# The first stage of a decoder step in another fixed order: loads issued by GpSimd, squares, responses and first GLU weights placed elsewhere

## The chip, the cores and the metric

The kernel runs on one core of one Trainium2 chip. The metric is the device time of one execution in microseconds (us), the median of the runs; lower is better. Engines are named as in the profile: PE is TensorE (PEld its weight loads), DVE is VectorE, ACT is ScalarE, POOL is GpSimd, SP is SyncE. SPq, ACTq and POOLq are the three sequencers as issuers of DMAs; each has a DMA queue of its own, and all queues share 16 DMA engines.

## The reference, cut to what matters

One inference step over 320 tokens (256 of a prompt, 8 sequences of 8 samples), model width 1024. Layer 0 mixes with a state space model (S5), layer 1 with latent attention; each then attends into 256 memory tokens and applies an MLP. The change lies in the S5 mixer and in the keys and values of layer 0's memory, which the kernel computes beside it.

```python
abar_re = mag * jnp.cos(ai * dt); abar_im = mag * jnp.sin(ai * dt)
bbar_re = coef_re[..., None] * br - coef_im[..., None] * bi     # and bbar_im
bu_re = jnp.einsum('gnk,btgk->btgn', bbar_re, ug)               # ug: rms_norm(x), 64 groups of 16
# h[t] = abar * h[t-1] + bu[t], for every group and state
y = jnp.einsum('gkn,btgn->btgk', cr, h_re) - jnp.einsum('gkn,btgn->btgk', ci, h_im)
y = y.reshape(bsz, t, dm) + d_skip * u
z = jax.nn.gelu(y, approximate=False) @ w_glu
out = z[..., :dm] * jax.nn.sigmoid(z[..., dm:])
k = (rms_norm(mem_prompt) @ w_mem_k); v = (rms_norm(mem_prompt) @ w_mem_v)
```

## The kernel before, in words

The tokens are cut into 40 chunks of 8 (`NCH`; 32 of the prompt, one for each sample). Inside a chunk the S5 layer is a short convolution (its *responses*, spread into the triangular tile `tt`); between chunks the state runs on in a scan. The 64 groups are treated in four quarters `hq` of 16. The pieces are small functions inside `s5_scan`, and the list of their calls is the order of the stage:

- `load_x` loads x (`xc`) and C (`natc`); C is cut into rows of 64 numbers. `mem_load` loads the memory tokens (`mt`), `mem_block(j)` turns one eighth of them into `mnp`.
- `products(i)`, i from 0 to 15: 16 matmuls of `mnp` with a 512 KB piece of the key or value weights; four pieces `i` are in flight, `products(i)` issues the load of piece i + 4 on SP. `keys(g)`, `keys_turned(g)`, `keys_out(g)` and `values_out(g)` copy the results out of PSUM, turn them and send them off through two halves of a buffer `kvo` (shown as `wlo`).
- The squares of x (`squares(i)`, 8 of them) give the norm of x; `x_scaled(i)` applies it, `x_turned(n)` turns x into `U`.
- `turned('b', q)`, `turned_out('b', q, p)` turn B, and the same with `'c'` turns C (PSUM tile `bcps`, results `m_b` and `m_c`).
- `state_weights(hq, hh)` on DVE and `state_turned(hq, hh)` on PE and ACT make the weights from chunk to state (`rt`), `states(hq)` applies them (`sps`). `out_weights(hq, hh)` on DVE makes the weights from state to output (`ca`, `ct`).
- `responses(hq)` fills a PSUM tile `kps`; `responses_out(hq)` copies it to the only buffer `kk` with four instructions of ACT, adds a diagonal on POOL, and spreads it to `tt` with 8 DMAs on SP. `kk` is free again when these have landed.
- `scan(f)` and `scanned(f)` run the scan of half the groups on DVE and copy it to `HS`. `outputs(hq, half)` multiplies `tt`, `ca`, `ct` by `U` and `HS` into a PSUM tile `yps`; ACT copies that to `yc` or `yg`; `outputs_turned`, `outputs_high` and `outputs_low` make the GLU's input. The dense GLU follows; its weights come in chunks through `load_chunk` (DMA, then `whi` on ACT and `wlo` on DVE).

PSUM has three rings: `mm` of 4 tiles (`products`, turned keys), `tp` of 2 (turns), and `at` of 2, which `rps`/`dps`, `ups`, `sps`, `kps` and `yps` take in turn. A tile of a ring is free when its reader has copied it out.

`in_order` ties every instruction of `s5_scan` to the one traced before it on the same engine, so that PE, DVE, ACT and SP run the list as written; what is traced later (the GLU's chunks) is put between by the scheduler. An engine whose next instruction waits holds back all behind it, and a DMA issue that cannot go on holds its sequencer.

Of the kernel before, what the change touches and what calls it, by code (L numbers as in the profile page):

```python
# [88 lines left out]
class Trunk:  # L89
# [88 lines left out]
    def load_chunk(self, srcs, cols):  # L178

        nc = self.nc  # L180
        if self.chunks_ahead:
            return self.chunks_ahead.pop(0)
# [12 lines left out]
        return hi, lo  # L195

# [412 lines left out]
    def s5(self, mkv):  # L609
        sp, close_sp = self.open("s5")  # L610
        mn, close_mn = self.open("memn0", side="right")
        with self.in_order((mybir.EngineType.PE, mybir.EngineType.DVE, mybir.EngineType.Activation, mybir.EngineType.SP)):
# [7 lines left out]
    def glu_chunk(self, k0):  # L620
        Wv = self.I['w_glu'][0].rearrange("(k p) c -> p k c", p=128)
        return self.load_chunk([(lambda t, o=o: t.rearrange("p (k c) -> p k c", c=512)[:, :, o * 256:(o + 1) * 256],
                                 Wv[:, k0:k0 + 2, o * D:o * D + 256]) for o in range(2)], 1024)

    def glu_loads(self, group):
        if group == 1:
            self.keys_scaled()
# [30 lines left out]
    def s5_scan(self, sp, mkv, mn):  # L658
# [39 lines left out]
        def load_x():  # L698
            for i in range(2):
                cols = slice(i * D // 2, (i + 1) * D // 2)  # L700
                A.dma_start(xc[i * NCH:i * NCH + NC_P], I['x_prompt'][0].rearrange("(c s) d -> c s d", s=L)[:, :, cols])
                A.dma_start(xc[i * NCH + NC_P:(i + 1) * NCH], I['x_sample'][:, :, cols])
            for i, part in enumerate(('re', 'im')):
                for o in range(2):
                    A.dma_start(nat['c'][i * G:(i + 1) * G, :, o], I[f'ssm_c_{part}'][0])

# [8 lines left out]
        PQ.dma_start(cm, I['c_chunk'])  # L715
        self.mem_load(0, mkv)
# [88 lines left out]
        T2 = pp.tile([128, 8, G], F32, name="T2")  # L805
        U = sp.tile([128, G * NCH + 24], F32, name="U")
# [4 lines left out]
        V.memset(tts[0], 0.0)  # L811
# [22 lines left out]
        load_x()  # L834
# [18 lines left out]
        A.activation(tts[1].rearrange("p s u k -> p (s u k)"), tts[0].rearrange("p s u k -> p (s u k)"), AF.Copy)  # L853
# [25 lines left out]
        A.activation(nat['b'][:, :, 1], nat['b'][:, :, 0], AF.Copy)  # L879
# [15 lines left out]
        def turned_out(c, q, p):  # L895
            A.activation(mat[c].rearrange("p r g k -> p k r g")[:, q * 4:q * 4 + 4],
                         p.rearrange("p (k r g) -> p k r g", k=4, r=2), AF.Copy)

        keys(0)
# [7 lines left out]
        for i in range(L):  # L907
            squares(i)
# [16 lines left out]
        V.tensor_add(rev(QX), T1, T2)  # L925
        V.tensor_mul(T1, Y1[:, :L], cb(cor))
# [32 lines left out]
        state_weights(0, 0)  # L959
        p = [turned('c', 0), turned('c', 1)]  # L960
        turned_out('c', 0, p[0])
        turned_out('c', 1, p[1])
        keys(1)
        ps = at("rps")
        products(4, lambda: nc.tensor.matmul(ps[:2 * NCH, :L], cm, rn[:, 0], start=True, stop=True))
        A.activation(rn[:, 1], ps[:2 * NCH, :L], AF.Sqrt, bias=self.eps[:2 * NCH, 0:1], scale=1.0 / D)
        A.activation(rm[:, 1], rm[:, 0], AF.Sqrt, bias=self.eps[:, 0:1], scale=1.0 / D)
        p = [turned('c', 2), turned('c', 3)]
        turned_out('c', 2, p[0])
        turned_out('c', 3, p[1])  # L970
        state_turned(0, 0)
        a8n = sp.tile([128, 2, G], F32, name="a8n", tag="a8n", bufs=1)
        A.activation(a8n[:, 0], PR[:, 8], AF.Copy)
        A.activation(a8n[:, 1], PI[:, 8], AF.Copy)
        for t, v in ((X1, PI), (Y1, PR)):
            A.activation(t[bot], v[bot], AF.Copy, scale=-1.0)
        state_weights(0, 1)
        V.reciprocal(rC, rn[:, 1])
        V.reciprocal(rm[:, 0], rm[:, 1])
# [13 lines left out]
        for i in range(4):  # L993
            x_scaled(i)
        products(5)
        state_turned(0, 1)
        for i in range(4, L):
            x_scaled(i)
        state_weights(1, 0)
        keys(2)  # L1000
        PQ.tensor_mul(dn, dn, gxn[:G])
# [5 lines left out]
        products(6)  # L1007
        V.tensor_copy(dT, ps[:K, :G])
        V.tensor_copy(rB, ps[:, 128:384])
        state_turned(1, 0)  # L1010
        state_weights(1, 1)
        keys_turned(0)
        for n in range(4):
            x_turned(n)
        state_turned(1, 1)
        for n in range(4, 8):
            x_turned(n)
        close_par()
# [1056 lines left out]
```

## Time and profile before

| | |
|---|---|
| time, median of 3 runs | 1228.91 us (1224.6 to 1232.43) |
| the profiled execution: time, span | 1227.92 us, 1226.3 us |
| PE busy over the span | 1131.8 us (92%) |
| DVE, ACT, POOL busy | 701.9, 555.9, 65.8 us |
| chain that ended last | PE 82%, ACT 6%, DVE 6%, DMA 3% |

The span is what the trace covers, and the time has 1.6 us more around it. The chain that ended last is read from the end back, each piece to what released it. "Idle before" names what an engine waited for.

### The profile page before, as it was taken

Reading aid. Unit: us, or ns where it says so; the run is one execution under the profiler, and the core shown is the slowest. Engines: PE = TensorE matmul, PEld = TensorE weight load, DVE = VectorE, ACT = ScalarE, POOL = GpSimd, SP = SyncE. Lnnn points to the kernel's source line nnn. Section 1 sums busy time; section 2 is a strip of 40 time slices with the busy share of each in tenths; the row PEclk is TensorE's granted clock in tenths of the full one; section 3 lists DMA queues with packets and bytes.
Section 4 is the critical chain, followed back from the end, with each engine's and each line's share of the span. In section 5 each row is a group of like instructions: output and inputs, shape, how many; then the busy total and the mean of one; then the engine's idle time right before and its main releaser. Section 6 shows DMA issues by size and latency. Waiting matters only on the chain.

```text
span 1226.3 us, 21300 instructions
## 1 busy us (share of the span) xinstructions
PE 1131.8 (92%) x8233; PEld 1025.4 (84%) x8233; DVE 701.9 (57%) x1327; ACT 555.9 (45%) x1012; POOL 65.8 (5%) x110
## 2 busy tenths in 40 slices
PE   2898869999899999999999999999998999999995
PEld 1787669986598999999988985569966899999995
DVE  2787944494358643564587584326852675335553
ACT  2764545444345543453375353324443465335531
POOL 0011100000000000000000054200000000000000
PEclk7998979999999999999999999989999999999998
DMA  8235259755434444554462654537561434444541
GB/s 203 87 83 138 36 130 292 272 189 189 174 118 130 152 155 143 150 154 148 147 186 74 171 179 139 168 137 248 182 232 61 137 109 149 146 148 139 168 141 43
DMA packets 152738, 185.38 MB, mean 151 GB/s; under 512 B 19824, under 2 KB 120445, under 8 KB 152573
## 3 DMA queue, kind: packets, MB, share of 16 engines
q1 hardware_dynamic: 140812, 173.00, 45.9%
q10 hardware_dynamic: 8592, 5.47, 1.9%
q0 software_dynamic: 3232, 5.55, 1.4%
q8 instruction: 65, 1.06, 0.4%
q14 instruction: 37, 0.30, 0.1%
HBM read 175.41 MB, written 6.21 MB: 148 GB/s over the span
## 4 chain that ended last, share of the span: by engine, by line
PE 82%; ACT 6%; DVE 6%; DMA 3%; issue 1%; SPq 1%; POOL 0%; POOLq 0%; ACTq 0%; DVEq 0%
PE mm L218 19%; PE mm L217 19%; PE mm L219 19%; PE mm L742 2%; PE kt L102 2%; PE sps L1451 2%; PE s L1934 2%; ACT whi L192 2%; PE ops L1466 1%; PE pov L1508 1%; PE s L1975 1%; DMA natc<-in_ssm_c_re 1%; DVE wlo L193 1%; PE ltp L102 1%; PE pps L1486 1%
## 5 line engine op out<-in xcount | busy, mean ns | idle before, releaser
L193 DVE TENSOR_TENSOR wlo<-wraw,whi 128x1024 fp32r<-128x1024 f32 (+1 forms) x216 | 260.0, 1206 | 291.4 <-ACT whi L192 271.8
L192 ACT ACTIVATE whi<-wraw 128x1024 fp32r<-128x1024 f32 (+1 forms) x216 | 224.4, 1045 | 309.4 <-PE mm L218 252.1
L218 PE MATMUL mm<-xl,whi 128*128 128x320 f32 x944 | 292.6, 313 | 1.6 <-DVE xl L294 1.0
L217 PE MATMUL mm<-xh,whi 128*128 128x320 f32 x944 | 279.7, 315 | 7.2 <-ACT xh L1478 4.5
L219 PE MATMUL mm<-xh,wlo 128*128 128x320 f32 x944 | 281.4, 312 | 0.1
L217 PEld LDWEIGHTS mm<-xh,whi 128*128 128x128 f32 x944 | 174.9, 190 | 9.8 <-ACT xh L1478 5.0
L218 PEld LDWEIGHTS mm<-xl,whi 128*128 128x128 f32 x944 | 179.6, 190 | 3.2 <-DVE xl L294 1.7
L219 PEld LDWEIGHTS mm<-xh,wlo 128*128 128x128 f32 x944 | 176.4, 190 | 0.3 <-DVE wlo L193 0.3
L217 PE MATMUL mm<-hh,whi 128*128 128x320 f32 x512 | 158.0, 309 | 0.0
L218 PE MATMUL mm<-hl,whi 128*128 128x320 f32 x512 | 158.0, 309 | 0.0
L219 PE MATMUL mm<-hh,wlo 128*128 128x320 f32 x512 | 157.1, 308 | 0.0
L218 PEld LDWEIGHTS mm<-hl,whi 128*128 128x128 f32 x512 | 96.1, 188 | 0.0
L217 PEld LDWEIGHTS mm<-hh,whi 128*128 128x128 f32 x512 | 96.1, 188 | 0.0
L219 PEld LDWEIGHTS mm<-hh,wlo 128*128 128x128 f32 x512 | 95.9, 188 | 0.0
L102 PE MATMUL kt<-ident,kn 128*128 128x128 f32 x256 | 37.5, 280 | 5.5 <-ACT ktb L1378 2.8
L102 PEld LDWEIGHTS kt<-ident,kn 128*128 128x128 f32 x256 | 27.8, 141 | 17.4 <-DVE ktb L1376 5.6
L1863 POOL DMA_DIRECT2D rop<-in_cache_k_rope x64 | 34.5, 538 | 37.3 <-issue 9.9
L118 DVE TENSOR_TENSOR sq<-sq 128x320 f32<-128x320 f32 x67 | 32.4, 483 | 2.3 <-ACT sq L120 1.6
L1567 DVE TENSOR_TENSOR t_up<-t_up 128x320 f32<-128x320 f32 x64 | 29.8, 486 | 2.1 <-ACT hh L1566 1.9
L1568 DVE TENSOR_TENSOR hl<-t_up,hh 128x320 fp32r<-128x320 f32 x64 | 29.8, 487 | 0.9
L1376 DVE COPY ktb<-kt 128x512 f32<-128x512 f32 x32 | 22.0, 688 | 12.4 <-PE kt L102 11.9
L1566 ACT ACTIVATE hh<-t_up 128x320 fp32r<-128x320 f32 x64 | 28.4, 471 | 0.9
(493 smaller groups left out, 1806.0 us busy)
## 6 DMA issues: line engine op xcount, KB each, us to landing
wraw<-in_w_mlp_up SPq DMA_DIRECT2D x64, 512.0 KB, 3.6
wraw<-in_w_mlp_down SPq DMA_DIRECT2D x64, 512.0 KB, 3.4
kn<-in_cache_mem_k SPq DMA_DIRECT2D x16, 1024.0 KB, 7.2
vn<-in_cache_mem_v SPq DMA_DIRECT2D x16, 1024.0 KB, 9.3
wraw<-in_w_glu SPq DMA_DIRECT2D x32, 256.0 KB, 4.0
wraw<-in_w_mem_q SPq DMA_DIRECT2D x16, 512.0 KB, 4.5
wraw<-in_w_mem_o SPq DMA_DIRECT2D x16, 512.0 KB, 4.2
lat<-in_cache_kv_latent SPq DMA_DIRECT2D x64, 128.0 KB, 2.2
```

What stands on the lines that cost most here:

```text
L102: return self.nc.tensor.transpose(out, in_, self.ident[b:b + k, b:b + k])
L118: eng.tensor_add(st['acc'], st['acc'], st['last'])
L192: nc.scalar.activation(hi[:, :cols], raw[:, :cols], AF.Copy)
L193: nc.vector.tensor_sub(lo[:, :cols], raw[:, :cols], hi[:, :cols].bitcast(F32))
L217: nc.tensor.matmul(ps, wh, xh, start=start, stop=False)
L218: nc.tensor.matmul(ps, wh, xl, start=False, stop=False)
L219: nc.tensor.matmul(ps, wl, xh, start=False, stop=stop)
L742: nc.tensor.matmul(o, w[:, bs], mnp[:, k, :], start=k == 0, stop=k == KD - 1)
L1566: A.activation(hh[b // 4][:, b % 4, :], a, AF.Square)
L1567: V.tensor_mul(a, a, a)
L1568: V.tensor_sub(hl[b // 4][:, b % 4, :], a, hh[b // 4][:, b % 4, :].bitcast(F32))
L1863: last[eng] = eng.dma_start(dst, src[bass.ds(v, 1)].rearrange("o p d -> (o p) d"))
```

## The change

- x and C are issued by POOL (software queue), x right after the small loads and C behind a small multiplication of `dn`; before, ACT issued them, between `mem_block(0)` and the sine.
- Four of the `squares` stand between the squares of the memory and the copy of B, four more between the two halves of B; the root follows there. C is turned later, after x is scaled, and gets its sign for the lower half in the copy from PSUM (`scale=sign`); `out_weights` and X1, Y1 no longer apply it. The second `tt` is cleared by DVE, no longer copied by ACT. `dT` and `rB` are copied by ACT, the start of the long powers by DVE from `PR` and `PI`.
- The list from `state_weights(0, 0)` to `outputs(1, 1)` is written anew: `responses(0)` earlier, `responses(1)` after the scan and its copy-out between the two halves of `outputs(0, ...)`, `products` 4 to 11 and the turned keys at other places, `yc` of quarter 1 in another pool.
- The first GLU chunk is loaded before `responses(3)` and split after `final_states`; `keys_scaled` is tied to the end of the stage; POOL is in order too.

```diff
+    def load_raw(self, srcs):
         raw = self.wtile('raw', F32)
         for shaper, src in srcs:
-            self.last_w = nc.sync.dma_start(shaper(raw), src)
+            self.last_w = self.nc.sync.dma_start(shaper(raw), src)
+        return raw
+
+    def split_chunk(self, raw, cols):
...
-                A.dma_start(xc[i * NCH:i * NCH + NC_P], I['x_prompt'][0].rearrange("(c s) d -> c s d", s=L)[:, :, cols])
...
-                    A.dma_start(nat['c'][i * G:(i + 1) * G, :, o], I[f'ssm_c_{part}'][0])
...
+            PQ.dma_start(xc[i * NCH:i * NCH + NC_P], I['x_prompt'][0].rearrange("(c s) d -> c s d", s=L)[:, :, cols])
+            PQ.dma_start(xc[i * NCH + NC_P:(i + 1) * NCH], I['x_sample'][:, :, cols])
+        PQ.tensor_mul(dn, dn, gxn[:G])
+        for i, part in enumerate(('re', 'im')):
+            for o in range(2):
+                PQ.dma_start(nat['c'][i * G:(i + 1) * G, :, o], I[f'ssm_c_{part}'][0])
...
         mem_block(0)
-        load_x()
         mem_block(1)
...
+        for i in range(4):
+            squares(i)
+        A.activation(nat['b'][:, :, 1], nat['b'][:, :, 0], AF.Copy)
         keys(0)
...
+        for i in range(4, L):
+            squares(i)
         p = [turned('b', 2), turned('b', 3)]
...
+        state_weights(0, 0)
+        for i in range(L):
+            x_scaled(i)
+        keys(1)
...
+        c_turned(0)
+        products(4)
+        state_weights(0, 1)
+        state_turned(0, 0)
...
+        products(5)
+        keys(2)
+        state_weights(1, 1)
+        state_turned(1, 0)
...
+        states(0)
         out_weights(0, 0)
+        state_turned(1, 1)
+        states(1)
         out_weights(0, 1)
-        states(0)
-        states(1)
+        products(6)
+        initial_states()
         long_powers()
         V.memset(H[:, :, :, 0], 0.0)
+        keys_turned(0)
+        responses(0)
+        responses_out(0)
...
-        products(10)
+        responses(1)
         scanned(0)
+        keys_out(2)
         outputs(0, 0)
+        responses_out(1)
         outputs(0, 1)
...
         values_out(6)
+        glu = self.glu_load(0)
         responses(3)
...
         outputs(2, 0)
-        self.chunks_ahead = [self.glu_chunk(0)]
-        values_out(7)
         outputs(2, 1)
+        final_states()
+        self.chunks_ahead = [self.split_chunk(*glu)]
+        values_out(7)
```

The order of the instructions shows three places. The first is ACT near the start of the program: `mnp` is the first memory block, `W` the sine and its half angle, `sq` the squares of the memory and of x. Before:

```order
L794 ACTIVATE mnp<-mps,gmT 128x256
L701 DMA xc<-in_x_prompt 32x8x512
L702 DMA xc<-in_x_sample 8x8x512
L701 DMA xc<-in_x_prompt 32x8x512
L702 DMA xc<-in_x_sample 8x8x512
L705 DMA natc<-in_ssm_c_re 64x16x64 x2
L705 DMA natc<-in_ssm_c_im 64x16x64 x2
L836 ACTIVATE W<-W 128x64
L837 ACTIVATE W<-W 128x64
```

and now:

```order
L802 ACTIVATE mnp<-mps,gmT 128x256
L847 ACTIVATE W<-W 128x64
L848 ACTIVATE W<-W 128x64
L802 ACTIVATE mnp<-mps,gmT 128x256 x3
L863 ACTIVATE sq,r_mem<-mt 128x1024 x2
L893 ACTIVATE sq,rn<-xc 80x512 x4
L910 ACTIVATE natb<-natb 128x16x64
```

The eight DMA issues between the first memory block and the sine have left ACT, and squares of x stand ahead of the copy of B.

The second place is ACT around the outputs of quarter 0 (`yps_1006`, `yps_1032` before, `yps_981`, `yps_1022` now) and the copies of the second responses (`kk_944` before, `kk_1007` now). Before:

```order
L1112 ACTIVATE kk_776<-kps_743 16x8x64 x4
L1112 ACTIVATE kk_944<-kps_911 16x8x64 x4
L782 ACTIVATE wlo_139<-mm_791,r_mem_114 128x256
L782 ACTIVATE wlo_139<-mm_792,r_mem_114 128x256
L769 ACTIVATE wlo_139<-kps_959,r_mem_114 128x256 x2
...
L1190 ACTIVATE wlo_138<-yps_1006 128x8x64
L1190 ACTIVATE wlo_138<-yps_1032 128x8x64
```

and now:

```order
L790 ACTIVATE wlo_148<-mm_790,r_mem_114 128x256
L790 ACTIVATE wlo_148<-mm_791,r_mem_114 128x256
L777 ACTIVATE wlo_148<-kps_802,r_mem_114 128x256 x2
...
L777 ACTIVATE wlo_148<-kps_931,r_mem_114 128x256 x2
L1193 ACTIVATE wlo_147<-yps_981 128x8x64
L1114 ACTIVATE kk_1007<-kps_936 16x8x64 x4
L1193 ACTIVATE wlo_147<-yps_1022 128x8x64
```

The second copies of `kk` have moved from behind the first ones to between the two halves of the outputs, and a pair of `keys_out` copies stands just ahead of the first half.

The third place is ACT at the end of the stage, where the GLU's chunks (`whi`) meet the outputs of quarter 2 (`yg`) and 3 (`yc`). Before:

```order
L192 ACTIVATE whi_1804<-wraw_1801 128x1024
L1190 ACTIVATE yg_1580<-yps_1609 128x8x64
L192 ACTIVATE whi_1866<-wraw_1863 128x1024
L1190 ACTIVATE yc_1627<-yps_1628 128x8x64
L1206 ACTIVATE yg_1580<-ytp_1646 128x80x4
```

and now:

```order
L193 ACTIVATE whi_1865<-wraw_1862 128x1024
L1193 ACTIVATE yg_1582<-yps_1601 128x8x64
L193 ACTIVATE whi_1631<-wraw_1396 128x1024
L790 ACTIVATE wlo_148<-mm_1539,r_mem_114 128x256
L790 ACTIVATE wlo_148<-mm_1540,r_mem_114 128x256
L193 ACTIVATE whi_1803<-wraw_1800 128x1024
L1193 ACTIVATE yc_1638<-yps_1639 128x8x64
```

`wraw_1396` is the chunk that is loaded early. The row ahead of the second `yg` copy still splits a chunk whose load stands behind the `gn` loads on SP, the second such pair, as before; the early chunk, the last values and one more chunk now stand between that copy and `yc`.

## Rows read from the trace of the kernel before

**Rows 1.** Windows: five stretches; busy us (instructions) per engine, granted clock, DMA share, GB/s.

```profile
0.00:27.58 27.58, 4.27 (x18) 3.26 (x18) 5.43 (x22) 4.16 (x8) 2.69 (x9) 0.78 0.90 206
27.58:72.92 45.34, 39.95 (x220) 34.20 (x220) 35.32 (x67) 37.24 (x76) 2.50 (x5) 0.91 0.33 99
72.92:134.87 61.95, 56.23 (x773) 49.02 (x774) 52.61 (x130) 30.13 (x79) 8.56 (x11) 0.94 0.38 89
134.87:175.40 40.53, 26.22 (x234) 22.66 (x233) 28.27 (x96) 18.02 (x36) 6.02 (x6) 0.83 0.53 110
175.40:1226.30 1050.90, 1005.14 (x6994) 916.23 (x6992) 580.30 (x1014) 466.37 (x816) 46.06 (x81) 0.98 0.50 157
```

**Rows 2.** Timeline of ACT, 9 to 31 us: start, duration, what [idle before].

```profile
13.10 5.55 ACTq L705 DMA_DIRECT2D natc<-in_ssm_c_re  x2
18.69 8.85 ACTq L705 DMA_DIRECT2D natc<-in_ssm_c_im  x2
27.58 0.26 ACT L836 ACTIVATE W<-W 128x64 f32<-128x64 f32 x1 [17.93 <-DMA natc<-in_ssm_c_re]
```

**Rows 3.** DMA issues of 5.5 to 6.0 us; then two windows, columns as Rows 1.

```profile
whi<-in_w_mem_k SPq DMA_DIRECT2D x1, 512.0 KB, 8.4
...
4.00:18.00 14.00, 4.27 (x18) 3.26 (x18) 3.30 (x14) 2.47 (x5) 0.21 (x1) 0.91 1.04 297
...
16.00:28.00 12.00, 0.00 (x0) 0.00 (x0) 0.13 (x1) 0.42 (x3) 0.00 (x0) 0.50 0.99 162
```

**Rows 4.** The tile hn, POOL's loads in rows of 64 numbers: durations, starts, landing.

```profile
L1040 POOL DMA_DIRECT2D hn<-in_cache_ssm_re x2: 592/620/647, 66.4 to 67.0; - x2
L1040 POOL DMA_DIRECT2D hn<-in_cache_ssm_im x2: 584/584/584, 67.6 to 68.2; - x2
...
DMA to landing us min/median/max: 2.7/3.7/4.2
```

**Rows 5.** Timeline of PE, 28 to 48 us.

```profile
28.88 5.50 PE L742 MATMUL mm<-mnp,wraw 128*128 128x256 f32 x16
34.22 3.62 PE L742 MATMUL mm<-mnp,whi 128*128 128x256 f32 x16
37.67 1.04 PE L102 MATMUL bcps<-ident,natb 128*128 128x128 f32 x8
```

**Rows 6.** Groups of ACT by line, 28 to 175 us: busy us, mean ns, idle before.

```profile
L1112 ACT ACTIVATE kk<-kps 16x512 f32<-16x512 f32 x16 | 9.4, 590 | 18.2 <-DMA tt<-kk 16.2 <-issue 1.2 <-PE kps L1106 0.7
L957 ACT ACTIVATE rt<-rps 128x512 f32<-128x512 f32 x16 | 8.8, 601 | 1.4 <-PE rps L102 1.4
L984 ACT ACTIVATE xr<-xc,rC 80x512 f32<-80x512 f32 x8 | 5.1, 712 | 0.0
L884 ACT ACTIVATE sq<-xc 80x512 f32<-80x512 f32 x8 | 5.0, 630 | 0.2
L896 ACT ACTIVATE m_b<-bcps 128x512 f32<-128x512 f32 x4 | 3.9, 1076 | 2.4 <-PE bcps L102 2.4
...
L990 ACT ACTIVATE U<-ups 128x320 f32<-128x320 f32 x8 | 3.1, 440 | 0.6 <-PE ups L102 0.5
L749 ACT ACTIVATE kt<-mm 128x256 f32<-128x256 f32 x8 | 2.8, 382 | 2.6 <-PE mm L742 2.5
...
L966 ACT ACT_TABLE_LOAD x1 | 1.3, 1283 | 0.0
```

**Rows 7.** One PE group, columns as Rows 6.

```profile
L744 PE MATMUL mm<-wraw,mnp 128*128 128x256 f32 x64 | 17.5, 435 | 5.3 <-ACT wlo L782 5.3
```

**Rows 8.** Timelines of ACT and of SP, 134 to 175 us.

```profile
134.87 2.39 ACT L1112 ACTIVATE kk<-kps 16x512 f32<-16x512 f32 x4 [1.20 <-issue]
...
164.62 1.06 ACT L192 ACTIVATE whi<-wraw 128x1024 fp32r<-128x1024 f32 x1 [5.22 <-DMA wraw<-in_w_glu]
...
167.54 1.06 ACT L192 ACTIVATE whi<-wraw 128x1024 fp32r<-128x1024 f32 x1 [1.13 <-DMA wraw<-in_w_glu]
...
161.07 12.40 SPq L185 DMA_DIRECT2D wraw<-in_w_glu  x10
```

More of the change, by code (lines that the diff above doesn't have):

```diff
@@ L611, in s5 @@
         mn, close_mn = self.open("memn0", side="right")
-        with self.in_order((mybir.EngineType.PE, mybir.EngineType.DVE, mybir.EngineType.Activation, mybir.EngineType.SP)):
+        with self.in_order((mybir.EngineType.PE, mybir.EngineType.DVE, mybir.EngineType.Activation, mybir.EngineType.SP, mybir.EngineType.Pool)):
             close_s8 = self.s5_scan(sp, mkv, mn)
@@ L618, in s5, with glu_load @@
         close_sp()
-    def glu_chunk(self, k0):
+    def glu_load(self, k0):
         Wv = self.I['w_glu'][0].rearrange("(k p) c -> p k c", p=128)
-        return self.load_chunk([(lambda t, o=o: t.rearrange("p (k c) -> p k c", c=512)[:, :, o * 256:(o + 1) * 256],
-                                 Wv[:, k0:k0 + 2, o * D:o * D + 256]) for o in range(2)], 1024)
+        return self.load_raw([(lambda t, o=o: t.rearrange("p (k c) -> p k c", c=512)[:, :, o * 256:(o + 1) * 256],
+                               Wv[:, k0:k0 + 2, o * D:o * D + 256]) for o in range(2)]), 1024
     def glu_loads(self, group):
         if group == 1:
-            self.keys_scaled()
+            with self.tc.issue_after(self.s5_last.ins):
+                self.keys_scaled()
         if group < 4:
@@ L805, in s5_scan @@
         T2 = pp.tile([128, 8, G], F32, name="T2")
+        sign = sp.tile([128, 1], F32, name="sign")
         U = sp.tile([128, G * NCH + 24], F32, name="U")
@@ L810, in s5_scan @@
         V.memset(U[:, G * NCH:], 0.0)
-        V.memset(tts[0], 0.0)
+        for hs, v in ((top, 1.0), (bot, -1.0)):
+            V.memset(sign[hs], v)
+        for t in tts:
+            V.memset(t, 0.0)
         A.activation(W[:, 9, 0:1], self.eps[:, 2:3], AF.Exp)
@@ L906, in s5_scan @@
         turned_out('b', 3, p[1])
-        for i in range(L):
-            squares(i)
+        ps = at("rps")
+        nc.tensor.matmul(ps[:2 * NCH, :L], cm, rn[:, 0], start=True, stop=True)
+        A.activation(rn[:, 1], ps[:2 * NCH, :L], AF.Sqrt, bias=self.eps[:2 * NCH, 0:1], scale=1.0 / D)
+        A.activation(rm[:, 1], rm[:, 0], AF.Sqrt, bias=self.eps[:, 0:1], scale=1.0 / D)
         products(3)
@@ L957, in state_turned @@
                 A.activation(rt[:, hh, half * 4:half * 4 + 4], ps.rearrange("p (x c) -> p x c", x=4), AF.Copy)
[L959 to L979, printed above, removed]
         UG = U[:, :G * NCH].rearrange("p (g c) -> p g c", c=NCH)
@@ L991, in x_turned, with c_turned @@
                          ps[:, :NT].rearrange("p (g h c) -> p g h c", h=2, c=NCH), AF.Copy)
-        for i in range(4):
-            x_scaled(i)
[L995 to L1001, printed above, removed]
+        def c_turned(h):
+            p = [turned('c', h), turned('c', h + 1)]
+            turned_out('c', h, p[0])
+            turned_out('c', h + 1, p[1])
+        state_weights(0, 0)
+        for i in range(L):
+            x_scaled(i)
+        keys(1)
         ps = at("dps")
@@ L1006, in s5_scan @@
         dT = sp.tile([K, G], F32, name="dT")
[L1007 to L1012, printed above, removed]
+        A.activation(dT, ps[:K, :G], AF.Copy)
+        A.activation(rB, ps[:, 128:384], AF.Copy)
+        c_turned(0)
+        products(4)
+        state_weights(0, 1)
+        state_turned(0, 0)
         for n in range(4):
             x_turned(n)
-        state_turned(1, 1)
+        state_weights(1, 0)
+        state_turned(0, 1)
+        c_turned(2)
         for n in range(4, 8):
             x_turned(n)
+        products(5)
+        keys(2)
+        state_weights(1, 1)
+        state_turned(1, 0)
+        a8n = sp.tile([128, 2, G], F32, name="a8n", tag="a8n", bufs=1)
+        a8r = sp.tile([128, 5, 2, 32], F32, name="a8r")
+        a8i = sp.tile([128, 5, 2, 32], F32, name="a8i")
+        for hs, gs in ((top, slice(0, 32)), (bot, slice(32, 64))):
+            V.tensor_copy(a8r[hs, 0, 0], PR[hs, 8, gs])
+            V.tensor_copy(a8i[hs, 0, 1], PI[hs, 8, gs])
         close_par()
@@ L1280, in s5_scan @@
         state_turned(2, 1)
-        products(11)
         keys_out(3)
-        values_out(5)
+        products(10)
         states(2)
@@ L1286, in s5_scan @@
         state_turned(3, 0)
-        outputs(1, 0)
-        outputs(1, 1)
+        products(11)
+        values_out(5)
         state_weights(3, 1)
@@ L1291, in s5_scan @@
         states(3)
+        outputs(1, 0)
+        outputs(1, 1)
         outputs_turned(0)
@@ L1314, in s5_scan @@
         outputs(2, 0)
-        self.chunks_ahead = [self.glu_chunk(0)]
+        outputs(2, 1)
+        final_states()
+        self.chunks_ahead = [self.split_chunk(*glu)]
         values_out(7)
-        outputs(2, 1)
         outputs(3, 0)
```

45 lines of the change are left out of this document (15 added, 30 removed).

## The prediction

> **What bounds the kernel now.** I read the windows first [rows 1]. From 175.4 us on PE is busy in 1005.1 of 1050.9 us: the GLU and all behind it are bound by PE, and the change touches only small pieces there, so I expect that part to start earlier or later and not to change its length. The first 175.4 us are another matter. PE is busy in 4.3 of the first 27.6 us, in 40.0 of the next 45.3, in 56.2 of the next 62.0 and in 26.2 of the last 40.5. So I ask for each of these four stretches which wait ends last.
>
> Start to 27.58. The sine of the S5 layer stands behind eight DMA issues on ACT. The four for C occupy ACTq from 13.10 to 27.54, and the sine starts at 27.58 after 17.93 us without work [rows 2]. DVE and PE stand still for as long, since the powers of A and five of the eight memory blocks stand behind it. Meanwhile the granted clock falls to 0.50 [rows 3], that is 1.2 GHz, and the first `products` take 5.50 us where the next take 3.62 [rows 5].
>
> 27.58 to 72.92. ACT is the fullest engine, 37.2 of 45.3 us [rows 1]; PE and DVE wait for its copies.
>
> 72.92 to 134.87 (first state matmuls to the copy of the third responses). PE is nearly full; its one large wait is 5.3 us for a copy of values [rows 7], which stood behind the second `kk` copies, and these waited for the spread of the first responses from the same buffer: the 16 copies have 16.2 us of such waits in all [rows 6].
>
> 134.87 to 175.40. This is a chain of issues: `kk` copied at 134.87, spread by SP, fourth responses, spread again, nine `gn` loads, then the GLU's chunks from 161.07, the second pair of which has landed when ACT splits at 167.54 [rows 8]. The outputs' copy that PE waits for is the next on ACT. PE starts the GLU at 175.40.
>
> **The change, part by part.** Times are against the profiled execution (1227.92 us; 1.0 below the median of the runs). I walk the new order with durations of the trace and note the same four marks.
>
> Mark 1, the turn of B on PE, is at 37.67 now [rows 5]. With the DMA issues gone from ACT the sine follows the first memory block, at some 10 us. What ends last is then the data. Ahead of the turn must have landed: memory 1.05 MB, two weight pieces 1.05, B 0.52, x 1.31, together 3.93 MB. From 4 to 18 us the DMA engines moved 297 GB/s at a share of 1.04, so they were full [rows 3]; at that rate 3.93 MB take 13.2 us, to 17.2. I add 0.4 for what the pieces behind take meanwhile: 17.6. Then 3.6 us of `products(1)`: the turn starts at 21.2, which saves 16.5 us. The other way to it is no longer: x by 15 to 16, then four squares (2.5 [rows 6]) and the copy of B. Bounds: the second piece landed at 5.7 + 8.4 = 14.1 now [rows 3], before x competed, which would save 3.5 more; and the engines stay full until 28 [rows 3], which would cost 10.4. The eight issues on POOL I take at 0.6 us each, as those for `hn` [rows 4], or four times that for C's, which have four times as many rows, if the time goes with the rows; that would still issue the last by 17 us. The copy of `tt` on ACT becomes a DVE memset in DVE's idle start, worth 0; `dT`, `rB` and the sign cost what they cost elsewhere.
>
> The Trainium skill ("DMA: Bandwidth & Descriptors", section "Queues, rings and completion order") says that each DMA engine takes turns between its queues packet by packet. By it x, which now starts early, would take its turns beside the weights and push the second piece back by up to its own 1.31 MB, 4.4 us at the rate above, from 14.1 to 18.5, and the sum would save 0.9 less. No row of the kernel before separates the two queues.
>
> Mark 2, the first `states`, is at 72.92 now, 35.3 us after mark 1. In the new order ACT has between them: two `keys` 1.5, B out of PSUM 3.9, four squares 2.5, the root's table 1.3, x scaled 5.1, C out of PSUM as B 3.9, two `rt` pairs 2.4, `U` 3.1 [rows 6], and some 1.5 for six small ones (an estimate): 25.2, with 0.5 for the turns between ACT and PE. PE starts `products(5)` a little before the last `U` copy ends, 3.6, and turns the next weights, 1.0 [rows 5]. So 30.3 us, mark 2 at 51.5: 5.0 saved. Taken out of this stretch are four of the squares, two turns of weights, and `products(6)`.
>
> Mark 3, the third `kk` copy, is at 134.87 now, 62.0 us after mark 2. What left the last stretch comes in here: `products(6)` 3.6, one turn of keys 0.5, one of weights 1.0: +5.1. PE's wait of 5.3 us goes, since the first `tt` is spread long before the second copy. New waits: the second half of `outputs(0, ...)` takes the PSUM tile of the second responses, since the ring `at` has two, and its copy-out is now behind the first half on ACT: four copies of 0.59 [rows 6] plus the first half's copy, 3.0 us of PE. The scan's copy to HS and a copy of keys, whose buffer half waits for the values' store, come just ahead: 1.0. The last turn of quarter 1 waits behind ACT's copies: 1.5. `products(8)` waits for `keys(3)`: 0.4. In sum +5.7, so 67.7 us, mark 3 at 119.2. Bounds for the new waits: 0, if DVE or ACT is ahead of my walk, and 8. DVE's rows do not bind here: 52.6 of 62.0 us busy [rows 1], nothing added but the wait for the root, which ends before its first weights are wanted.
>
> Mark 4, the GLU, is 40.5 us after mark 3 now. That chain of SP is kept: the early chunk is issued while SP would wait for the fourth responses, and is hidden there. It does not end the wait, because the row ahead of the second `yg` copy still splits a chunk that is loaded behind the `gn` loads, the second pair as before [rows 8]. The early chunk's split, a copy of values and one more split now stand ahead of `yc`: 1.9 us, of which PE's work hides all but some 0.4. `keys_scaled`, four DVE instructions, falls into DVE's gap after the last lows; without that cover it would cost up to some 3 us (an estimate).
>
> Sum: 16.5 + 5.0 - 5.7 - 0.4 = 15.4 us saved, the GLU at 160.0, and 1227.9 - 15.4 = 1212.5. I say **1212**.
>
> **The rivals.** *The new waits don't bite.* The 5.9 us of PSUM and copy waits are read from a walk whose parts may be off against each other by as much. Without them 1206.6; with the weights landing as early as now, 1203. For it speaks that ACT is busy only 30 of 62 us there [rows 1].
>
> *The loads share evenly.* If all that is queued lands together at 28, mark 1 is at 31.6, and the time is 1223. For it speaks the share of 0.99 up to 28 [rows 3]; against it, that C is behind x on one queue and the later pieces behind the first on the other.
>
> *The software queue is slow for short rows.* This one ends slower. `hn`, four loads of 64 KB in rows of 256 bytes, took from 66.4 to 68.2 + 3.7 = 71.9 [rows 4], 262 KB in 5.5 us, 48 GB/s. If that were a rate and not mostly the fixed delay of a landing, x and C, 2.36 MB, would need 49 us and land at 53. PE turns C at about 31, ACT could copy it at 37, and up to 34 the delay is free; so 19 us would be lost against 15.4 won, and 1.9 more by the first `products` behind the gap at 1.2 GHz [rows 5]: 1227.9 + 5.5 = 1233. It decides once C lands after 49 us. Against it: each of the four landed in 2.7 to 4.2 us, whether first or last, so they flowed together.
>
> The Trainium skill ("DMA: Bandwidth & Descriptors", section "Issuing engine by pattern") speaks against the change: it calls loads issued by SP or ACT generally faster than those by GpSimd. By that rule 1233 would be nearer; no row shows the same load on both queues.
>
> **How the numbers follow.** Chances: the forecast, 1207 to 1217, 0.47; new waits that don't bite, 1200 to 1207, 0.24; loads that share, 1217 to 1226, 0.20; the software queue, 1226 to 1245, 0.09. Leaving out the lowest and the highest tenth or so gives 1202 to 1224. One per cent (12.3 us) is about what a measurement of this kernel can tell from no change; its line is at 1216.6 below and 1241.2 above. Faster: 0.24 + 0.45 = 0.69; slower 0.04; the same 0.27.
>
> **What would show it.** Right: the sine at about 10 us and no DMA issue on ACT between it and the first memory block; the turn of B near 21, the first `states` near 51, the third `kk` copy near 119, the GLU near 160; PE waiting some 3 us for ACT's second `kk` copies between the halves of quarter 0; ACT waiting for a `wraw` of the GLU ahead of a `yg` copy. Wrong: squares of x or the turn of C waiting for POOL's loads beyond 25 and 34 us; PE in the third stretch held by DVE; a GLU stretch longer than 1051 us.

## The result, and the profile after

The kernel after took 1215.08 us, median of four runs (1214.25 to 1218.76); the kernel before took 1230.67 beside it (1224.60 to 1233.01, four runs). The ratio is 0.9887 with a 95% interval of 0.9843 to 0.9930: 1.1% faster. The forecast was 1212 in a range of 1202 to 1224. The profiled execution took 1214.25 us, 13.7 less than that of before.

The total was about right, by luck: its parts were not. These are the four marks of the prediction and the end of the span, in us:

| | before | predicted | after | saved in the stretch up to it: predicted | measured |
|---|---|---|---|---|---|
| turn of B | 37.67 | 21.2 | 30.55 | 16.5 | 7.1 |
| first `states` | 72.92 | 51.5 | 59.32 | 5.0 | 6.5 |
| third `kk` copy | 134.87 | 119.2 | 123.12 | -5.7 | -1.85 |
| GLU | 175.40 | 160.0 | 162.46 | -0.4 | 1.2 |
| end of the span | 1226.30 | 1210.9 | 1212.60 | 0 | 0.8 |

The windows of after, cut at its own marks, answer to [rows 1]; columns as there. Three of the first stretch alone stand below them.

```profile
0.00:30.55 30.55, 14.43 (x52) 11.92 (x53) 17.90 (x63) 12.23 (x27) 8.27 (x17) 0.83 0.90 220
30.55:59.32 28.77, 24.45 (x158) 20.73 (x156) 23.02 (x30) 24.86 (x51) 3.31 (x5) 1.00 0.27 84
59.32:123.12 63.80, 58.90 (x802) 51.76 (x802) 57.86 (x141) 32.24 (x82) 7.01 (x10) 1.00 0.42 102
123.12:162.46 39.34, 26.17 (x233) 22.16 (x233) 19.36 (x78) 17.73 (x36) 5.12 (x6) 0.87 0.49 99
162.46:1212.60 1050.14, 1006.19 (x6994) 916.91 (x6992) 583.83 (x1019) 465.76 (x816) 46.67 (x81) 0.98 0.50 158
...
4.00:18.00 14.00, 4.70 (x20) 3.82 (x20) 11.08 (x44) 6.38 (x14) 5.47 (x9) 0.93 1.03 231
16.00:20.00 4.00, 0.00 (x0) 0.00 (x0) 1.41 (x6) 1.80 (x5) 0.00 (x0) 0.52 1.04 207
20.00:24.00 4.00, 3.18 (x8) 2.58 (x9) 0.00 (x0) 1.09 (x4) 0.00 (x0) 0.50 1.03 225
```

The last stretch is as long as before, 1050.1 against 1050.9 us (the 0.8 is within what it scatters, see below), so what was won was won ahead of the GLU. In the first stretch the DMA engines are as full from 4 to 18 us as before (share 1.03, 1.04 in [rows 3]), but move 231 GB/s where they moved 297.

The timelines of ACT and PE in after (start, duration, what, idle before it) answer to [rows 2], [rows 5] and [rows 8].

```profile
9.94 0.25 ACT L847 ACTIVATE W<-W 128x64 f32<-128x64 f32 x1
...
18.14 0.63 ACT L893 ACTIVATE sq<-xc 80x512 f32<-80x512 f32 x1 [3.32 <-DMA xc<-in_x_sample]
...
123.12 2.39 ACT L1114 ACTIVATE kk<-kps 16x512 f32<-16x512 f32 x4 [1.20 <-issue]
...
154.74 1.06 ACT L193 ACTIVATE whi<-wraw 128x1024 fp32r<-128x1024 f32 x1 [11.27 <-DMA wraw<-in_w_glu]
155.70 0.58 ACT L1193 ACTIVATE yg<-yps 128x512 f32<-128x512 f32 x1
```

```profile
20.82 6.44 PE L750 MATMUL mm<-mnp,wraw 128*128 128x256 f32 x16 [8.30 <-DMA wraw<-in_w_mem_k]
27.10 3.62 PE L750 MATMUL mm<-mnp,whi 128*128 128x256 f32 x16
30.55 1.04 PE L102 MATMUL bcps<-ident,natb 128*128 128x128 f32 x8
...
156.33 1.97 PE L102 MATMUL ytp<-ident,yg 128*128 128x128 f32 x8 [7.61 <-ACT yg L1193]
```

The sine comes at 9.94 where it came at 27.58: the order does what it says. PE then waits for the first weight piece until 20.82, its clock is at 0.52 from 16 to 20 us and at 0.50 from 20 to 24, that is 1.2 GHz, and the first `products` take 6.44 us.

### The profile page after: what moved, and what is told of

It is laid out like the page before. It is cut to its first block, busy times and chain, and to the rows that moved or that the text cites. A ratio compares the mean times of both kernels' runs of the same rounds, so it can differ in the third digit from the quotient of the medians.

```text
span 1212.6 us, 21296 instructions
## 1 busy us (share of the span) xinstructions
PE 1130.1 (93%) x8233; PEld 1023.5 (84%) x8233; DVE 702.0 (58%) x1328; ACT 552.8 (46%) x1009; POOL 70.4 (6%) x118
## 4 chain that ended last, share of the span: by engine, by line
PE 79%; ACT 7%; DMA 5%; issue 4%; DVE 2%; SPq 2%; POOL 0%; POOLq 0%; ACTq 0%; DVEq 0%
PE mm L224 19%; PE mm L225 19%; PE mm L226 19%; PE kt L102 2%; ACT whi L193 2%; PE sps L1458 2%; PE s L1941 2%; DMA wraw<-in_w_mem_q 2%; PE mm L750 1%; DMA wraw<-in_w_mem_k 1%; DMA wraw<-in_w_glu 1%; PE ops L1473 1%; PE pov L1515 1%; PE s L1982 1%; SPq L1122 1%
```

## The experiments

The stretches up to the GLU are compared by the four marks of each profile (turn of B, first `states`, third `kk` copy, GLU), always given in this order. A mark is read from one profile. Five kernels with the same loads in the same order have the turn of B at 30.20 to 30.55 us (after, sq_all, glu_hold31, kk_hold, best3). The first `states` scatter more: glu_hold31 and kk_hold have the same list up to there and are 2.9 us apart. The part from the GLU to the end took between 1046.5 and 1054.9 us in the fourteen profiles (before, after and twelve experiments), so of a total only differences above some 4 us are read as the work of an edit.

### Who issues the loads

**act_loads**: the kernel after, with the loads of x and C back on ACT behind the first memory block.

```diff
-            PQ.dma_start(xc[...], I['x_prompt']...)        # GpSimd, at the start
-                PQ.dma_start(nat['c'][i * G:(i + 1) * G, :, o], I[f'ssm_c_{part}'][0])
+            A.dma_start(xc[...], I['x_prompt']...)         # ACT, ahead of the sine
+                A.dma_start(nat['c'][i * G:(i + 1) * G, :, o], I[f'ssm_c_{part}'][0])
```

> The changed kernel with the loads of x and C issued by ACT again, at their old place between the first two memory blocks; all else as changed. Theory 'the move of the loads frees the sine, and that is the gain of the first stretch': the sine is back at about 27.6 us, the turn of B at 37 to 40 instead of 30.55, the stretches behind keep their length, and the time is 7 to 9 us above the changed kernel's, near 1222. Rival 'the first stretch is bound by data that land near 25 us in either form': the turn of B stays under 33 and the time rises by under 3 us.

Measured: 1228.80 us, ratio 0.9986 (0.9958 to 1.0013); marks 36.16, 67.7, 132.88, 172.72. ACT's timeline shows the old stall again:

```profile
13.43 4.12 ACTq L845 DMA_DIRECT2D natc<-in_ssm_c_re  x2
...
18.89 7.33 ACTq L845 DMA_DIRECT2D natc<-in_ssm_c_im  x2
26.27 0.26 ACT L847 ACTIVATE W<-W 128x64 f32<-128x64 f32 x1 [16.44 <-DMA natc<-in_ssm_c_re]
```

With the loads on ACT the new order alone is worth 1.0 us of 1229.84, which its interval doesn't tell from none; by the GLU's mark it is 2.7. The gain needs the loads away from their old place on ACT, between the first memory block and the sine; x may stay on ACT if it is issued at the start (x_act, below).

**before_loads** does the opposite: the kernel before, with nothing changed but who issues these loads (`A.dma_start` becomes `PQ.dma_start` in the same two places, and `load_x()` is called at the start).

> The kernel before with one thing changed: the loads of x and C are issued by GpSimd at its start. Theory 'the loads are the change': putting them back on ACT in the changed kernel gave 1228.8, within 2 us of the kernel before, so moving them alone takes the kernel before to 1214 to 1219. Rival 'loads and order need each other': in the old order the gain of the first stretch is lost again behind it, and the time is 1222 or more.

Measured: 1221.97 us, ratio 0.9932 (0.9907 to 0.9957); marks 30.30, 65.50, 127.14, 170.59. The turn of B is where after has it, and the GLU is 4.8 us earlier than before, 8.1 later than after. By that mark the loads alone bring 4.8 us, the order alone 2.7 and both 12.9, so 5.4 us belong to neither alone (by the medians 8.0, 1.0 and 15.6, which leaves 6.6). Without the loads ACT stands still whatever its order; without the order the squares and the second responses stand where they stood.

### What holds the first stretch

After has its B at 30.55, 9.4 us behind the forecast. The suspects are C's loads, x's loads, GpSimd's queue, and ACT's list.

**c_held**: C's loads wait behind a one-column copy on GpSimd that reads the second weight piece; x starts at once.

```diff
+        PQ.tensor_copy(seen[:, 0:1], raws[1][:, 0:1])
         for i, part in enumerate(('re', 'im')):              # moved down, behind load(3)
             for o in range(2):
                 PQ.dma_start(nat['c'][i * G:(i + 1) * G, :, o], I[f'ssm_c_{part}'][0])
```

> The changed kernel with C's four loads on GpSimd behind a small GpSimd copy that reads the second weight piece, so that C is asked for only when that piece has landed; x is asked for at once, as now. Theory 'x and C take turns with what SP asked for, and C's short rows slow all of them': without C the first piece lands at 12 to 15 us instead of 20.7, the second by 18, the turn of B is at 21 to 24, C has landed by 30, ahead of its turn, and the time falls by 6 to 9 us to about 1207. Rival 'x alone does it': the first piece lands at 18 or later and the turn of B stays at 28 or later, with under 2 us gained.

Measured: 1215.22 us, ratio 0.9892 (0.9840 to 0.9945); marks 27.59, 57.35, 122.26, 161.49. DVE, which takes B as soon as it has landed, and GpSimd:

```profile
20.99 1.93 DVE L889 TENSOR_TENSOR natb<-bn,gxn 128x1024 f32<-128x1024 f32 x1 [3.31 <-DMA bn<-in_ssm_b_im]
```

```profile
22.04 0.81 POOL L729 COPY seen<-whi 128x1 f32<-128x1 f32 x1 [15.68 <-DMA whi<-in_w_mem_k]
```

B lands at 20.99, where in after it lands at 25.79; the second weight piece is there by 22.04, and the first `products` start at 19.10, 1.7 earlier than in after. C's loads cost the landing of B 4.8 us and its turn 3.0, since here `products` end last; the rest is there without them. Of the 3.0 us 1.0 is left at the GLU, and the total doesn't show it (1215.22 against 1215.08).

**xc_held**: x waits behind the first piece and C behind the second, in the same manner.

```diff
+        PQ.tensor_copy(seen[:, 0:1], raws[0][:, 0:1])      # then x's loads
+        PQ.tensor_copy(seen[:, 1:2], raws[1][:, 0:1])      # then C's loads
```

> As the kernel with C held back, and x held back too, behind a small GpSimd copy that reads the first weight piece. Theory 'taking turns': the first piece lands at 11 to 13 us and the second by 15, the first products start by 13 and run at the full clock, but x lands at 18 or later, four squares (3.2 us) and the copy of B (1.1) stand behind it, so the turn of B is at 21 to 24 again and the time is that of the kernel with C alone held back, within 3 us. Rival 'order of the loads does not matter, the sum of bytes does': B still lands near 25 and the turn of B stays at 28 or later.

Measured: 1214.90 us, ratio 0.9878 (0.9830 to 0.9927); marks 29.92, 63.1, 128.61, 168.18. Timelines of GpSimd, PE and ACT:

```profile
11.11 0.19 POOL L724 COPY seen<-wraw 128x1 f32<-128x1 f32 x1 [7.42 <-DMA wraw<-in_w_mem_k]
```

```profile
12.02 3.62 PE L753 MATMUL mm<-mnp,wraw 128*128 128x256 f32 x16
15.47 3.62 PE L753 MATMUL mm<-mnp,whi 128*128 128x256 f32 x16
29.92 1.97 PE L102 MATMUL bcps<-ident,natb 128*128 128x128 f32 x8 [10.82 <-ACT natb L913]
```

```profile
25.93 0.63 ACT L896 ACTIVATE sq<-xc 80x512 f32<-80x512 f32 x1 [11.34 <-DMA xc<-in_x_sample]
```

With x and C held back the first piece is there at 11.1 and both products have run by 19.1, at full clock: x and C did take the weights' turns in after. But x now lands at 25.9, the squares of x stand ahead of the copy of B on ACT, and B is turned no earlier. The transfer that was late has changed places; the stretch is as long. The GLU comes 5.7 us later than in after, and the total is the same: its last stretch is the shortest of all, 1046.5 us.

**x_act**: c_held, with x on ACT's hardware queue from the start (`A.dma_start` behind the load of `gmn`), to tell GpSimd's queue from x itself.

> As the kernel with C alone held back, but x's four loads are issued by ACT at its start (its hardware queue) instead of by GpSimd, some 3 us of issues on ACT ahead of its first table load. Theory 'GpSimd's queue slows the DMA engines while it carries x': from 8 to 16 us the engines move 280 to 330 GB/s instead of about 195, the first piece lands by 16 us and the second by 18, the turn of B is at 21 to 24. Rival 'any second queue beside SP's does it': 190 to 220 GB/s there, the first piece lands near 19 and the turn of B is near 27.6 as with C held back.

Measured: 1212.01 us, ratio 0.9845 (0.9818 to 0.9873); marks 27.92, 57.69, 124.56, 163.81. PE's timeline:

```profile
19.49 5.14 PE L752 MATMUL mm<-mnp,wraw 128*128 128x256 f32 x16 [2.17 <-DMA wraw<-in_w_mem_k]
24.47 3.62 PE L752 MATMUL mm<-mnp,whi 128*128 128x256 f32 x16
```

Up to the first `states` that is c_held within 0.4 us, and from 4 to 18 us the DMA engines moved 227 GB/s in both. So the stretch isn't long because x is on GpSimd's queue; it is as long with x on ACT's. Inside it the two differ, so this is no clean test of the queues. In x_act SP's early loads come later: the first matmul is at 8.41 (4.77 in c_held), the first memory block is copied at 14.38 (9.74), and SP issues the second weight piece at 10.71 (5.78). And the turns are others; the DMA view of 12 to 16 us (SP's queue, then ACT's: packets, MB, share of 16 engines):

```profile
q1 hardware_dynamic: 433, 0.50, 55.6%
q10 hardware_dynamic: 257, 0.49, 54.1%
```

The profile is that of the slowest of four runs (1220.35 us), so the last two marks and the median do not go together.

**x_sp**: x on SP between the second and the third weight piece, C on GpSimd behind x.

```diff
         load(1)
+        nc.sync.dma_start(xc[...], I['x_prompt']...)       # and x_sample
         load(2)
+        PQ.tensor_copy(seen[:2 * NCH, 0:1], xc[:, L - 1, 0:1])   # then C's loads
```

> The changed kernel with x's four loads issued by SP behind the second weight piece and C's by GpSimd behind a small copy that reads x. Theory 'taking turns and the slow queue cost 9 us ahead of the turn of B': the first piece lands at 11 to 12 us, the second by 15, x by 18 to 19, four squares and the copy of B follow (4.3 us), the turn of B is at 22 to 24 instead of 30.55, the first states at 51 to 53, and the time falls by 5 to 8 us. Rival 'what follows takes it back' (C lands late, or the granted clock falls in the gaps that open): the first states stay at 57 or later and under 3 us are gained.

Measured: 1216.65 us, ratio 0.9877 (0.9836 to 0.9918); marks 28.18, 61.42, 126.21, 166.35. Windows, columns as in [rows 1]:

```profile
16.00:20.00 4.00, 3.93 (x19) 3.12 (x17) 3.86 (x9) 0.00 (x0) 0.00 (x0) 1.00 1.06 180
20.00:24.00 4.00, 0.00 (x0) 0.00 (x0) 3.82 (x10) 0.00 (x0) 0.00 (x0) 0.98 1.09 180
24.00:28.00 4.00, 0.00 (x0) 0.00 (x0) 1.27 (x2) 3.71 (x9) 3.63 (x5) 0.50 1.07 347
```

The first products start at 12.09 and the second at 16.31, but x lands at 24.2, and the copy of B stands behind its squares on ACT, as in xc_held. From 16 us until x has landed the engines are full at 180 GB/s; behind it, just as full, they move 347.

**sq_all**: the kernel after, with all eight squares ahead of the copy of B (`for i in range(4)` becomes `range(L)`, the second loop goes), to see whether ACT's list sets the second stretch.

> The changed kernel with all eight squares of x ahead of ACT's copy of B, where ACT waits 6.65 us for B anyway, instead of four there and four behind the copy of B out of PSUM. Theory 'between the turn of B and the first states ACT's list sets the end': the turn of B stays at 30 to 31, the first states come 2.5 to 3 us earlier, at 56 to 57, and the time falls by 1 to 3 us. Rival 'PE or DVE sets it': the first states stay within 1 us of 59.3.

Measured: 1218.22 us, ratio 0.9908 (0.9876 to 0.9940); marks 30.20, 58.71, 122.40, 161.88. Four squares, 3.0 us of ACT's work, went into ACT's wait, and the stretch got 0.3 us shorter (28.77 to 28.51). ACT's timeline says where they went:

```profile
35.17 1.91 ACT L905 ACTIVATE m_b<-bcps 128x512 f32<-128x512 f32 x2 [2.36 <-PE bcps L102]
```

ACT comes earlier and waits for the second half of B's turn, which stands on PE behind the third `products`. That ACT's list alone sets this stretch is refuted.

**best6** puts it all together: x_sp, the copy of B ahead of all squares, `products(3)` and the squares ahead of the root, and kk_hold (below).

> The kernel with x on SP behind the second weight piece and C behind x, the copy of B ahead of all squares of x, the third and fourth products ahead of the root's matmul, the second kk copies ahead of the outputs and the GLU splits behind them. Theory 'with x late it is the squares ahead of the copy of B that hold its turn': without them the turn of B is at 19.5 to 21 us instead of 28.2, ACT starts the squares when x lands near 24, the scaling of x starts at 32 to 34 instead of 39.8, the first states come at 52 to 55 and the time is 4 to 8 us below 1203.1. Rival 'PE's gaps pull the granted clock down and give it back': the first states stay at 57 or later and the time within 3 us of 1203.

Measured: 1208.15 us, ratio 0.9844 (0.9803 to 0.9885); marks 20.04, 62.04, 122.46, 154.73. PE's timeline:

```profile
20.04 1.10 PE L102 MATMUL bcps<-ident,natb 128*128 128x128 f32 x8 [0.20 <-ACT natb L910]
26.42 5.82 PE L752 MATMUL mm<-mnp,wraw 128*128 128x256 f32 x16 [5.29 <-DMA wraw<-in_w_mem_k]
32.08 1.04 PE L102 MATMUL bcps<-ident,natb 128*128 128x128 f32 x8
```

The first half of B is turned at 20.0, 1.2 us ahead of the forecast's mark, and nothing is won: the third weight piece, now behind x, lands at 26.4, the second half of B is turned at 32.1, and the first `states` come at 62.0, 2.7 later than in after and 0.2 later than in kk_hold.

**c_once**: kk_hold, with C loaded once, its second half copied by GpSimd in 1.04 us.

```diff
-            for o in range(2):
-                PQ.dma_start(nat['c'][i * G:(i + 1) * G, :, o], I[f'ssm_c_{part}'][0])
+            PQ.dma_start(nat['c'][i * G:(i + 1) * G, :, 0], I[f'ssm_c_{part}'][0])
+        PQ.tensor_copy(nat['c'][:, :, 1], nat['c'][:, :, 0])
```

> The kernel with the second kk copies ahead of the outputs and the GLU splits behind them (1203.11), with C loaded once (0.52 MB instead of 1.05) and its second half made by one GpSimd copy of 128 x 1024. Theory 'the DMA engines' work until about 28 us sets when the turn of B and what follows can start, whatever its order': 0.52 MB at some 200 GB/s less, so what ends last lands 2.5 us earlier, the turn of B is at 27.5 to 28.5 instead of 30.2 and the first states come 1.5 to 3 us earlier than 59.0, if the granted clock holds; the time is 1200 to 1203. Rival 'C was behind the weights anyway': the turn of B stays at 30 or later.

Measured: 1205.63 us, ratio 0.9829 (0.9772 to 0.9886); marks 28.16, 57.95, 118.74, 149.30. This is the one edit that takes data out of the stretch (0.52 MB) and does not reorder it, and B is turned 2.1 us and the GLU starts 5.1 us earlier than in kk_hold. Not all of the 5.1 is the edit's: at the first `states` c_once is 3.9 ahead of kk_hold, but only 1.1 ahead of glu_hold31, which has the same list up to there. The time is not below kk_hold's, since from the GLU on this profile has 1054.2 us where kk_hold has 1048.9. Whether those 5 us come from the edit stays open.

### The waits behind the first stretch

**glu_hold31**: the splits of the next three GLU pairs are placed behind the last copy of `yc`. In after the split at 154.74 stands ahead of the copy of `yg`, and PE waits 7.61 us for that copy.

```diff
+            self.y_copy[hq, half] = A.activation(ycs[hq]..., AF.Copy)
+        self.hold.update({self.chunk + i: self.y_copy[3, 1] for i in (1, 2, 3)})
```

> The changed kernel with the splits of the next three pairs of GLU weights queued on ACT behind the last copy of the outputs (yc of quarter 3), so that no split of a pair loaded behind the gn loads stands ahead of the second yg copy. Theory 'that split holds the outputs': the second yg copy is at about 149 instead of 155.7, PE's wait of 7.6 us for it goes, the GLU starts at 154 to 157 instead of 162.46 and the time falls by 5 to 8 us to about 1208. Rival 'the GLU's weights bind': PE then waits as long for the second pair inside the GLU, and under 2 us are gained.

Measured: 1209.27 us, ratio 0.9851 (0.9800 to 0.9902); marks 30.22, 59.01, 124.35, 154.58. The wait is gone and the GLU starts 7.9 us earlier than in after; 5.8 of it are in the total. So this chain was the bound of the fourth stretch, not the `gn` loads themselves. Another wait of after is still there, in PE's timeline:

```profile
92.77 0.44 PE L1190 MATMUL yps<-tt,U 128*64 128x128 f32 x4 [3.50 <-ACT wlo L1194]
```

**kk_hold**: glu_hold31, with `responses_out(1)` moved from between the halves of quarter 0 to behind `scanned(0)`, so that the second responses leave PSUM ahead of that quarter's first copy.

```diff
+        responses_out(1)      # behind scanned(0)
...
-        responses_out(1)      # between outputs(0, 0) and outputs(0, 1)
```

> The kernel with the GLU splits queued behind the outputs, and the second kk copies (responses 1) moved on ACT from between the halves of outputs(0) to behind the scan's copies, ahead of a keys copy. Theory 'the second half waits for the PSUM tile that these copies free': PE's wait of 3.2 us for ACT goes, the third kk copy comes 2.5 to 3.5 us earlier than in the kernel without this move, and the time is 2 to 4 us below its 1209.27. Rival 'the wait is made good later' (DVE, full in that stretch, ends last): the third kk copy comes under 1 us earlier and the time stays within 1.5 us.

Measured: 1203.11 us, ratio 0.9779 (0.9756 to 0.9802); marks 30.22, 61.88, 122.27, 154.41. The second copies now run at 89.30 in 2.38 us, the wait of 3.50 is gone, and the third stretch is 60.39 us against 65.34 in glu_hold31. The third stretch of glu_hold31, then of kk_hold, columns as in [rows 1]:

```profile
59.01:124.35 65.34, 60.56 (x802) 53.27 (x802) 57.88 (x141) 32.19 (x82) 7.01 (x10) 0.97 0.41 100
```

```profile
61.88:122.27 60.39, 58.75 (x803) 51.83 (x803) 55.74 (x134) 32.21 (x83) 8.52 (x10) 1.00 0.43 108
```

The 4.9 us are not the wait alone: behind it glu_hold31's clock is 0.72 from 92 to 96 us and 0.85 from 96 to 100, where kk_hold has 1.00, and PE is busy for 1.8 us more. (The move also let the scheduler bring SP's load of one more GLU pair forward, but that is issued at 132.70, behind this stretch.) The `states` come 2.9 later, in a profile whose clock is 0.52 from 48 to 56 us, where glu_hold31 has 1.00. PE was as idle ahead of it in both (busy for 1.9 of the 4 us from 44), so why the clock fell in one of them is open. This is the fastest of the kernels.

**best3**: sq_all and kk_hold together.

> All eight squares ahead of the copy of B, the second kk copies ahead of the outputs, and the GLU splits behind the outputs, together. Theory 'the three waits lie in different stretches and add up': 1203.1 less 1 to 3 us, 1200 to 1202. Rival 'ACT's gain ahead of the first states is filled again by DVE': 1203 to 1205.

Measured: 1204.26 us, ratio 0.9796 (0.9752 to 0.9840); marks 30.44, 60.71, 121.27, 153.88: the same as kk_hold, so the placing of the squares is worth nothing measurable beside it either.

## Why the time came out right and the first mark did not

**The step that failed** is the first term: "at that rate 3.93 MB take 13.2 us, to 17.2. I add 0.4 for what the pieces behind take meanwhile: 17.6." B landed at 25.79, and the second `products` started at 27.10. The mechanism held (ACT free, then the data ends last); its size did not, 7.1 us saved where 16.5 were forecast. DVE and ACT of after, then the queues of GpSimd and SP from 0 to 25.79 us (packets, MB, share of 16 engines):

```profile
25.79 1.94 DVE L887 TENSOR_TENSOR natb<-bn,gxn 128x1024 f32<-128x1024 f32 x1 [8.27 <-DMA bn<-in_ssm_b_im]
```

```profile
27.77 1.06 ACT L910 ACTIVATE natb<-natb 128x1024 f32<-128x1024 f32 x1 [6.65 <-DVE natb L887]
```

```profile
q0 software_dynamic: 896, 2.40, 44.8%
q1 hardware_dynamic: 2013, 2.84, 44.5%
```

The 8.2 us from 17.6 to 25.79 divide so:

- 3.5 for the rate: from 4 to 25.79 us the engines moved 235 GB/s, and 3.93 MB take 16.7 us, not 13.2.
- 4.5 for C, the term that was missing: the forecast put C behind what B needs, but when B lands GpSimd's queue has moved all 2.40 MB of its loads, C with them. C is 1.05 MB, 4.5 us at that rate; with C held back (c_held) B lands 4.8 us earlier.
- 0.2 stays unaccounted for.

From there to the turn the forecast had 3.6 us and after has 4.8. PE had stood still for 8.3 us and ran at 0.50, and the second `products` follow the start of the first by 6.28 us, not 3.6. But ACT's copy of B ends at 28.83, 1.7 ahead of the turn, so the low clock costs this mark 1.7 at most.

How the queues shared the engines, DMA views of 8 to 20 us, before and then after:

```profile
q1 hardware_dynamic: 1970, 2.33, 73.3%
q10 hardware_dynamic: 449, 0.87, 34.9%
```

```profile
q0 software_dynamic: 590, 1.77, 73.5%
q1 hardware_dynamic: 569, 0.69, 31.6%
```

In after GpSimd's queue and SP's go packet for packet, 590 to 569, but GpSimd's packets hold 3.0 KB on average and SP's 1.2, so x and C take 72% of the bytes, and SP's weights and B the rest. In the other kernels with x on GpSimd from the start the counts are as even (c_held 386 to 382 from 8 to 16 us). The Trainium skill ("DMA: Bandwidth & Descriptors", section "Queues, rings and completion order") says that a DMA engine goes round between its queues and drains a whole packet of one before it turns to the next. By that rule the trace agrees; the prediction, which drew on it, saw x alone take turns, not C. With x on ACT's queue the counts are not even (x_act, 433 to 257), and why is open.

The rival "the loads share evenly" put the first mark at 31.6, and 30.55 is nearer to it than to the forecast. Its time of 1223 did not come, because the other terms were too bad by 7.7 us together (0.8 of it in the last stretch, which is scatter):

**Mark 2** was 1.5 us too bad: 28.8 us where 30.3 were walked, with ACT busy 24.9 of them, as summed (25.2). The allowances for turns and for the last `products` were too large.

**Mark 3** was 3.9 us too bad. The waits of PE from 59.32 to 123.12 in after (us in total, times, longest):

```profile
PE yps L1189 <- ACT wlo L1193: 3.2, 1, 3.2
PE sps L1058 <- ACT rt L975: 0.9, 2, 0.7
PE yps L1192 <- ACT HS L1161: 0.6, 1, 0.6
PE yps L1192 <- ACT HS L1163: 0.2, 1, 0.2
```

The predicted PSUM wait of 3.0 is there with 3.2, the scan's with 0.8 for 1.0, the turn of quarter 1 with 0.7 for 1.5 (the other 0.2 of that row are a later quarter's); only `products(8)` waits for nothing (0.4). The term that was missed is what the removed wait had cost behind it. In before, PE's timeline and the window from 100 to 104 us:

```profile
98.73 6.47 PE L744 MATMUL mm<-wraw,mnp 128*128 128x256 f32 x16 [5.28 <-ACT wlo L782]
```

```profile
100.00:104.00 4.00, 4.00 (x10) 3.11 (x10) 3.90 (x5) 1.71 (x4) 1.44 (x3) 0.50 0.87 144
```

After its 5.28 us the clock was 0.50, and the 16 products took 6.47 us where 16 take 3.62 at full clock: 2.9 more. So +5.1 moved in, -5.3 for the wait, -2.9 for its clock, +4.9 for the four waits: +1.8, and 1.85 were measured. (The 5.1 are the forecast's, and 0.5 us of small waits in before are left out, so the sum is good to some half a microsecond.) The rival "the new waits don't bite" falls.

**Mark 4** was 1.6 us too bad, with the wait as described: the split behind a `w_glu` pair ahead of the `yg` copy, 7.61 us of PE.

**The rival of the slow queue** falls. C's four loads landed 13.0 to 17.1 us after their issue at 6.3 to 8.8, so by 26 us at the latest; PE turns C from 40.2. The Trainium skill ("DMA: Bandwidth & Descriptors", section "Issuing engine by pattern") calls loads by SP or ACT generally faster. In the time that these loads took of the engines the traces do not bear it out: from 0 to 45 us x and C took 28.8% of 16 engines for 2.37 MB on ACT's queue in before, and 25.7% for 2.40 MB on GpSimd's in after, 13.0 against 11.6 us of all engines. What moved beside them was not the same in the two.

**What bounds the first 60 us.** Up to the turn of B it is the bytes that go ahead of B: with C alone held back (c_held, x_act) or loaded once (c_once) the turn comes 2.1 to 3.0 us earlier than in the kernel without that edit. Where x was put later too, B or the weights came earlier and x was the last (xc_held, x_sp), or a later piece (best6). The first `states` came between 57.4 and 63.1 us in the eleven kernels in the new order with x and C away from their old place on ACT, whichever transfer was last. That it is the sum of the bytes and not x's slow transfer (180 GB/s in x_sp) is argued: no run loads x in another form. That a smaller load brings the turn of B forward was shown (c_once); its worth in the whole time was not.

## What to carry to other kernels

Where full DMA engines set a start, name the bytes that must land ahead of each step and the queue that they share turns with: here the queue with the larger packets took 72% of the bytes, C among them, which nobody waited for yet. Putting one transfer later can make it the last, as x was in xc_held and x_sp. When a wait is taken out, look at the duration of the instructions right behind it too, since a wait of TensorE may have been paid twice, once in idle time and once at the lower clock. Compare marks along the path and not the total alone: here two errors of 9.4 and 7.7 us nearly cancelled in it, which was luck.

## What the runs showed of the hardware

In x_sp the DMA engines, full throughout, moved 180 GB/s from 16 us until x had landed at 24.2, and 347 from 24 to 28. Its loads go to 32 and to 8 partitions in rows of 2 KB; whether that is the cause was not tried.

C's loads, in rows of 256 bytes, held ACT for 5.55 and 8.85 us a pair [rows 2]. GpSimd issued the same two pairs in 1.67 and 1.62 us, and the sine was free.

After TensorE had idled for 5.28 us (before), 5.29 (best6) and 8.30 (after), the granted clock was 0.50 and the same 16 products took 6.47, 5.82 and 6.44 us against 3.62 at full clock: the price doesn't grow with the idle time. In c_held they took 5.19 us behind 6.42 of idle, and in act_loads 5.31 behind 15.21 (with two turns between), although the granted clock stands at 1.00 all the while; why they were slow there is open.
